# Stick-breaking attention in four steps, the tokens' memory attention beside the gate, and one more FFN part by block products

## The chip, the cores and the metric

One core of a Trainium2 chip runs the whole program. The metric is the device time of one execution in microseconds (us), and lower is better. TensorE (PE in the profile) does the matrix products and the transposes, VectorE (DVE) and ScalarE (ACT) the elementwise work, GpSimd (POOL) little; SyncE (SP) issues nearly all DMAs. Each engine runs its own instructions in a fixed order and waits at the first whose data or buffer is not ready.

## The reference

A decoder step of two layers with shared weights, for 1024 prompt tokens and 8 sample tokens, all in float32. Layer 0 mixes tokens with a gated linear recurrence (HGRN2), layer 1 with stick-breaking attention over keys and values that are projected after layer 0. Both have four heads of cross-attention to 256 memory tokens beside it, and a SwiGLU FFN of hidden width 2816.

```python
def swiglu(h, w_gu, w_down):
    gate, up = jnp.split(h @ w_gu, 2, axis=-1)
    return (jax.nn.silu(gate) * up) @ w_down

# stick-breaking, for a block of queries
z = einsum('bqhd,bkhd->bhqk', q, k) * scale + bias
log_keep = where(mask, log_sigmoid(-z), 0.0)
tail = cumsum(log_keep, axis=3, reverse=True) - log_keep
w = where(mask, exp(log_sigmoid(z) + tail), 0.0)
o = einsum('bhqk,bkhd->bqhd', w, v)

# memory attention
p = softmax(einsum('blhd,bmhd->bhlm', q, mk) * scale)
o = einsum('bhlm,bmhd->blhd', p, mv)

# each sub-layer: h = h + rmsnorm(sublayer(rmsnorm(h, g)), g')
```

The outputs are the tokens of both kinds after the two layers, the recurrent states, and the keys and values.

## The kernel before

Tokens lie along the free dimension. The prompt is done in two groups of 512; the second group takes the 8 sample tokens along, so that its tiles are 520 wide (as halves of 256 and 260 columns in the FFN). A float32 product is made of three: operand and weight are each split into a high and a low half (ACT casts, line L217 or L612; DVE subtracts, L218 or L614), and high x high, high x low and low x high are summed in PSUM. So each 512 columns of weights cost a DMA, a cast and a subtraction before PE can use them.

A scheduler sets the order of the instructions on each engine from the program's order and its buffers. The program's order is made by streams (generators) that `weave((stream, n), ...)` runs side by side, in proportion to the numbers n. `tc.issue_after` ties one instruction behind another.

The FFN's hidden width is done in five parts of 5, 5, 4, 4 and 4 slices of 128 columns (parts 0 to 4, so that the fourth part is part 3). A plain slice (`gate_up_q`, L545) takes 96 matmuls of half the group's width. In `ffn_w` a slice takes seven block products (`gate_up_w`, L619) in the way of Strassen, 84 matmuls, from sums of operand blocks (`sums_w`, done once for a group) and sums of weight blocks (made in DRAM by GpSimd's DMAs, `wsum`, or on the spot). The list `steps` given to `ffn_w` says how many slices stay plain, and how many steps of the operand sums go beside each of them. For the first group of layer 0 that list was (5, 6, 5): the first three slices of part 3 were plain, its last one and part 4 used block products.

Stick-breaking (`sb_prompt`) goes head by head over units of at most 512 scores by 128 queries, in steps: scores (L1594), softplus and reverse scan (L1580, L1581, L1614, L1616), the exponential of the weights (L1617), transposes of them (`turn`, L1623) and the values (L1634). One call of `step` begins a unit, turns the unit before it and takes the values of the one before that:

```python
old, turned = turned, asked and (*asked[0], *turn(*asked[1]))
asked = new
if old:
    values(*old)
```

Memory attention (`mem_attn`) has the same form with a softmax (L1051, L1019, L1032). The names in the profile: `ws` split weights, `w` and some `b` and `c` tiles raw weights, `x`, `a`, `y` split operands or their sums, `q` and `s` PSUM banks of FFN products and of small work (three banks), `m` the FFN's middle. Pool C holds four tiles of 2 x 512 columns, pool B seven of 512.

The stages that the change touches, with their times in the profile: samples' recurrence, gate and FFN part 1 of layer 0's first group (507 to 620 us); memory attention of the tokens and of the samples beside part 2 (to 700); parts 3 and 4 (to 865); layer 1 of the first group, stick-breaking and memory attention beside parts 0 and 1, some of them by block products (975 to 1195); layer 1 of the second group beside layer 0's FFN (1526 to 1840); and the end (from 2368).

## Time and profile before

| | us |
|---|---|
| median of 3 runs | 2404.62 (2404.50 to 2404.99) |
| the profiled execution, as the runs are timed | 2406.1 |
| its span, first to last instruction | 2404.4 |
| PE busy | 2377.7 (99%) |
| DVE busy | 1710.3 (71%) |
| ACT busy | 1322.5 (55%) |
| POOL busy | 113.7 (5%) |

The prediction quotes the page and its views word for word. In a row of groups stand line, engine, operation, the tile written <- the tiles read, the shape and a count; then the busy time and the mean duration of one in ns; then the idle time of the engine before them and what ended it. In a row of waits stand who waited for whom, the total in us, how often, and the longest. A timeline's row begins with start and duration in us.

### The profile page before, as it was taken

How to read it: one execution, taken by the hardware profiler on the slowest of the kernel's cores; microseconds unless marked ns; L12 is line 12 of the kernel's file. 1: busy time of each engine (PE TensorE's matmuls, PEld its weight loads, DVE VectorE, ACT ScalarE, POOL GpSimd, SP SyncE). 2: the span in 40 equal slices, each digit the busy share in tenths (PEclk: the TensorE clock that was granted, in tenths of full speed). 3: DMA queues.
4: the chain of work that ended last, by engine and by line, in shares of the span. 5: the costliest groups of instructions: out<-in, count | busy, mean ns of one | idle time of the engine just before them, and what ended most of it. 6: DMA issues, size and time to landing. Idle time of an engine off the chain costs nothing.

```text
span 2404.4 us, 42487 instructions
## 1 busy us (share of the span) xinstructions
PE 2377.7 (99%) x15962; PEld 2156.4 (90%) x15962; DVE 1710.3 (71%) x3195; ACT 1322.5 (55%) x2736; POOL 113.7 (5%) x187
## 2 busy tenths in 40 slices
PE   9999999999999999999999999999999999999998
PEld 7888989888889988999999989877778989999998
DVE  5867558766776676878556677777776679676866
ACT  5547544454664554667544554568457566554445
POOL 1001202100000000000001200111000000000000
PEclk9999999999999999999999999999999999999999
DMA  6454766677535447332659746545354354343342
GB/s 198 122 165 119 174 199 161 164 197 193 168 106 166 134 154 232 94 101 88 193 168 225 205 152 194 161 137 156 108 154 125 95 158 137 106 129 100 113 125 76
DMA packets 514641, 357.60 MB, mean 149 GB/s; under 512 B 20173, under 2 KB 463674, under 8 KB 514434
## 3 DMA queue, kind: packets, MB, share of 16 engines
q1 hardware_dynamic: 498562, 312.93, 43.8%
q0 software_dynamic: 15872, 41.95, 7.4%
q8 instruction: 126, 2.06, 0.4%
q14 instruction: 81, 0.66, 0.1%
HBM read 322.86 MB, written 65.49 MB: 162 GB/s over the span
## 4 chain that ended last, share of the span: by engine, by line
PE 85%; DVE 6%; ACT 4%; DMA 3%; issue 2%; SPq 0%; DVEq 0%; ACTq 0%
PE mm L231 37%; PE q L619 18%; PE q L791 11%; PE q L545 4%; PE mm L1235 2%; PE s L1414 1%; DMA b<-qd 1%; PE s L1051 1%; PE s L1032 1%; PE mm L968 1%; PE mm L995 1%; PE q L823 1%; DVE ws L218 1%; ACT c L1123 1%; DVE b L1614 1%
## 5 line engine op out<-in xcount | busy, mean ns | idle before, releaser
L231 PE MATMUL mm<-x,ws 128*128 128x512 f32 (+1 forms) x5016 | 924.4, 342 | 2.2 <-ACT a L1470 1.1
L231 PEld LDWEIGHTS mm<-x,ws 128*128 128x128 f32 x5016 | 774.8, 188 | 111.4 <-ACT a L1470 1.3
L217 ACT CAST ws<-w 128x512 fp32r<-128x512 f32 x596 | 346.6, 584 | 396.1 <-PE mm L231 228.4
L218 DVE TENSOR_TENSOR ws<-w,ws 128x512 fp32r<-128x512 f32 x596 | 381.1, 646 | 238.5 <-ACT ws L217 230.5
L791 PE MATMUL q<-m,ws 128*128 128x260 f32 (+1 forms) x2496 | 303.9, 283 | 0.1
L791 PEld LDWEIGHTS q<-m,ws 128*128 128x128 f32 x2496 | 299.9, 188 | 1.0 <-ACT m L238 0.3
L619 PE MATMUL q<-y,ws 128*128 128x260 f32 (+1 forms) x1920 | 249.3, 284 | 1.9 <-DVE t L654 1.7
L619 PEld LDWEIGHTS q<-y,ws 128*128 128x128 f32 x1920 | 237.6, 188 | 3.2 <-DVE t L654 1.9
L619 PE MATMUL q<-x,ws 128*128 128x260 f32 (+1 forms) x1668 | 219.7, 283 | 1.3 <-DVE ws L614 0.7
L619 PEld LDWEIGHTS q<-x,ws 128*128 128x128 f32 x1668 | 207.7, 188 | 2.2 <-DVE ws L614 1.1
L231 PE MATMUL mm<-m,ws 128*128 128x512 f32 x768 | 186.1, 396 | 0.0
L612 ACT CAST ws<-w 128x512 fp32r<-128x512 f32 x206 | 125.0, 619 | 96.8 <-PE q L791 30.8
L231 PEld LDWEIGHTS mm<-m,ws 128*128 128x128 f32 x768 | 142.9, 188 | 32.0
L614 DVE TENSOR_TENSOR ws<-w,ws 128x512 fp32r<-128x512 f32 x206 | 139.4, 688 | 44.9 <-ACT ws L612 41.6
L800 DVE TENSOR_TENSOR r<-r,q 128x260 f32<-128x260 f32 (+1 forms) x160 | 60.6, 420 | 46.8 <-PE q L791 46.5
L545 PE MATMUL q<-x,ws 128*128 128x260 f32 (+1 forms) x720 | 87.0, 282 | 0.0
L545 PEld LDWEIGHTS q<-x,ws 128*128 128x128 f32 x720 | 86.3, 188 | 0.2
L238 ACT CAST m<-t 128x512 fp32r<-128x512 f32 (+1 forms) x88 | 54.7, 622 | 37.5 <-DVE t L860 19.8
L612 ACT CAST ws<-b 128x512 fp32r<-128x512 f32 x82 | 50.6, 620 | 42.5 <-PE q L791 13.4
L614 DVE TENSOR_TENSOR ws<-b,ws 128x512 fp32r<-128x512 f32 x82 | 56.5, 689 | 20.6 <-ACT ws L612 19.9
L239 DVE TENSOR_TENSOR m<-t,m 128x512 fp32r<-128x512 f32 (+1 forms) x88 | 60.9, 691 | 13.5 <-ACT m L238 12.5
L290 DVE TENSOR_TENSOR st<-st,n 128x512 f32<-128x512 f32 (+1 forms) x91 | 62.3, 692 | 3.7 <-ACT n L289 2.2
(422 smaller groups left out, 3117.0 us busy)
## 6 DMA issues: line engine op xcount, KB each, us to landing
w<-in_w_gu SPq DMA_DIRECT2D x275, 256.0 KB
w<-in_w_down SPq DMA_DIRECT2D x160, 256.0 KB
wsum<-in_w_gu POOLq DMA_DIRECT2D x48, 512.0 KB, 6.1
w<-in_w_in_a SPq DMA_DIRECT2D x80, 256.0 KB
w<-in_w_o SPq DMA_DIRECT2D x64, 256.0 KB
w<-wsum SPq DMA_DIRECT2D x61, 256.0 KB
b<-in_w_gu SPq DMA_DIRECT2D x39, 256.0 KB
b<-wsum SPq DMA_DIRECT2D x39, 256.0 KB
```

What stands on the lines that cost most here:

```text
L217: nc.scalar.copy(ws[:, 0, :n, :], raw[:, :n, :])
L218: split[0] = nc.vector.tensor_sub(ws[:, 1, :n, :], raw[:, :n, :], ws[:, 0, :n, :].bitcast(F32))
L231: nc.tensor.matmul(ps[:, a, : PW[g]], wt, xt[k][:, xi, o : o + PW[g]], start=(k == 0 and wi == 0), stop=(k == nk - 1 and wi == 2),)
L238: nc.scalar.copy(dst[0], src)
L239: nc.vector.tensor_sub(dst[1], src, dst[0].bitcast(F32))
L290: nc.vector.tensor_add(acc[:, :n], acc[:, :n], t[:, :n])
L545: ins = nc.tensor.matmul(pp[a][:, :h], wt, xt[k][:, xi, a * h : (a + 1) * h], start=(k == 0 and wi == 0), stop=(k == ND - 1 and wi == 2),)
L612: nc.scalar.copy(w[:, 0, :], src)
L614: split[0] = nc.vector.tensor_sub(w[:, 1, :], src, w[:, 0, :].bitcast(F32))
L619: nc.tensor.matmul(ps[:, :h], w[:, wj, k * P : (k + 1) * P], x[:, xi, :], start=(first and k == 0 and wi == 0), stop=(k == 3 and wi == 2), ...
L791: nc.tensor.matmul(pp[a][:, :h], wt, mids[k][:, xi, a * h : (a + 1) * h], start=(k == 0 and wi == 0), stop=(k == nf - 1 and wi == 2),)
L800: nc.vector.tensor_add(d, d, pp[a][:, :h])
```

## The change

Six things:

- **Block products.** `ffn_w` of layer 0's first group gets the empty list: all four slices of part 3 now use block products. The operand sums stand beside part 2, where the memory attention was.
- **Memory attention of the tokens** in layer 0's second group goes one stage earlier, beside the samples' recurrence, the gate and part 1. Since the tiles for its result do not exist yet, it is parked in the key tiles (`parked`) and moved later (`unpark`). The samples' memory attention is woven 8 steps beside part 2 and 24 beside parts 3 and 4.
- **Stick-breaking** turns a unit one step later, and its e tile is half a C tile (`spare`) instead of a B tile.
- **The samples' recurrence** goes by four samples in one C tile, not by eight in two.
- **The end**: the first half of the output rows is turned after product 5 and not 7, the last product is scaled by DVE into a tile of its own, and the rows are stored in halves of 256 KB.
- **Loads and pacing**: two of the residual's tiles are fetched first and the others as they are needed, and the splits in `mixer_b.load` are tied behind the last weight split.

```diff
-        po, asked, turned = [None, None], None, None
+        po, asked, scored, turned, spare = [None, None], None, None, None, []
         def step(new=None):
-            nonlocal asked, turned
+            nonlocal asked, scored, turned
             old, turned = turned, asked and (*asked[0], *turn(*asked[1]))
-            asked = new
+            asked, scored = scored, new
...
-            e = B()
+            if not spare:
+                c = C()
+                spare.extend((c[:, 0], c[:, 1]))
+            e = spare.pop(0)
...
-        for h in range(H):
+        for h, a in ((h, a) for h in range(H) for a in range(2)):
...
-            for a in range(2):
-                qs = B(F32R), B(F32R)
-                split_to(qs, vb[:, a, :])
-                late.extend((h, a, i, p) for i, p in enumerate(qs))
+            qs = B(F32R), B(F32R)
+            split_to(qs, vb)
+            late.extend((h, a, i, p) for i, p in enumerate(qs))
...
+        def mem_parked(self):
+            yield from mem_attn(self.g, 0, self.Qm, lambda h, po: nc.scalar.copy(self.parked(h), po))
+
+        def unpark(self):
+            for h in range(H):
+                put(self.xo, H + h, slice(0, G), self.parked(h))
+                yield
...
-                    nc.scalar.activation(R, R, AF.Copy, scale=gcol(l, 3, m))
-                    if m == 7:
-                        list(rows.turn(0))
+                    if m < ND - 1:
+                        nc.scalar.activation(R, R, AF.Copy, scale=gcol(l, 3, m))
+                    else:
+                        rows.last = T()[:, :h]
+                        nc.vector.tensor_scalar(rows.last, R, gcol(l, 3, m), None, op0=ALU.mult)
+                    if m == 5:
+                        rows.first()
...
+                    if c < CH:
+                        t0 = G + c * P
+                        nc.sync.dma_start(y_prompt[0, t0 : t0 + P, s], yt[:, s])
...
+    weave((a1.sample(), 16), (a1.gate(), 4), (a1.mem_parked(), 11), (f0.part(1), 14), (w0, 9))
     a1.open()
-    weave((a1.sample(), 16), (a1.gate(), 4), (f0.part(1), 14), (w0, 9))
-
-    def rest():
-        yield from f0.part(2)
-        set_banks(True)
-        fw = ffn_w(0, 0, o0.x, (5, 6, 5), 3, False, f0.R)
-        yield from fw.part(3)
-        yield from fw.part(4)
-        f0.acc = fw.acc
-
-    weave((chain(a1.merge(), a1.mem()), 36), (ms, 74), (rest(), 33))
+
+    fw = ffn_w(0, 0, o0.x, (), 3, False, f0.R)
+    weave((chain(a1.merge(), a1.unpark(), fw.sums), 25), (islice(ms, 8), 8), (f0.part(2), 15))
+    set_banks(True)
+    weave((ms, 24), (chain(fw.part(3), fw.part(4)), 20))
+    f0.acc = fw.acc
...
-    weave((chain(b0.sb(), b0.mem()), 25), (chain(fw.part(0), fw.part(1)), 28))
+    weave((chain(b0.sb(), b0.mem()), 26), (chain(fw.part(0), fw.part(1)), 28))
...
-        (chain(b1.sb(), b1.mem()), 40), (chain(b1.sb_sample(), b1.mem_sample()), 76),
+        (chain(b1.sb(), b1.mem()), 41), (chain(b1.sb_sample(), b1.mem_sample()), 76),
```

How the order moves is shown at two places. The first is PE in layer 1 of the second group (from some 1540 us), where the stick-breaking's scores (`s<-a,a`) and transposes (`s<-ident,b`) stand among the products of layer 0's FFN (`mm<-x,ws`). Before:

```order
L1594 MATMUL s_17240<-a_17122,a_16525 128x512
L1623 MATMUL s_17250<-ident,b_17129 128x128 x4
L231 MATMUL mm_17274<-x_16902,ws_17266 128x512 x3
L231 MATMUL mm_17274<-x_16906,ws_17266 128x512 x3
L231 MATMUL mm_17274<-x_16970,ws_17266 128x512 x3
L231 MATMUL mm_17274<-x_16974,ws_17266 128x512 x3
```

And now, from the second unit's scores on:

```order
L1621 MATMUL s_17296<-a_17178,a_16581 128x512
L231 MATMUL mm_17322<-x_16958,ws_17314 128x512 x3
L231 MATMUL mm_17322<-x_16962,ws_17314 128x512 x3
L231 MATMUL mm_17322<-x_17026,ws_17314 128x512 x3
L231 MATMUL mm_17322<-x_17030,ws_17314 128x512 x3
L231 MATMUL mm_17322<-x_17095,ws_17319 128x512 x3
L231 MATMUL mm_17322<-x_17099,ws_17319 128x512 x3
L231 MATMUL mm_17322<-x_17163,ws_17319 128x512 x3
L231 MATMUL mm_17322<-x_17167,ws_17319 128x512 x3
L1621 MATMUL s_17354<-a_17178,a_16581 128x512
L1653 MATMUL s_17364<-ident,b_17185 128x128 x4
```

The transposes of a unit stood right behind the next unit's scores; now 24 products and another unit's scores lie between.

The second place is layer 1 of the first group, at its first slice by block products (about 1010 us). SP's queue there, before (`ksc` and `vsc` are a head's keys and values in DRAM, `c` the raw weights of that slice, which had been loaded by four DMAs some 25 rows ahead; the `c` rows here are for the slices behind it):

```order
L1654 DMA a_1766_10852<-ksc1_151 128x512
L212 DMA w_1737_10641<-in_w_gu 128x4x128
L1655 DMA a_1767_10853<-vsc1_155 128x512
L212 DMA w_1739_10646<-in_w_gu 128x4x128
L212 DMA w_1745_10715<-in_w_gu 128x4x128
L212 DMA w_1747_10720<-in_w_gu 128x4x128
L579 DMA w_1758_10813<-in_w_gu 128x4x128
```

And now, where the first loads of `c` stand behind the keys of head 2:

```order
L585 DMA w_1808_11028<-in_w_gu 128x4x128
L1684 DMA a_1830_11187<-ksc2_152 128x512
L585 DMA c_1711_10358<-in_w_gu 128x4x128
L585 DMA c_1712_10359<-in_w_gu 128x4x128 x2
L585 DMA c_1711_10358<-in_w_gu 128x4x128
```

The load of the keys `ksc2` goes into the tile that held head 0's keys, so it waits for the last scores of that head. The loads of the weights stood ahead of all keys and now stand behind that wait.

ACT at the same place, before (`ws_1763` is the slice's first weight):

```order
L530 ACTIVATE t_1713_10468<-t_1713_10468 128x520
L217 CAST ws_1748_10722<-w_1747_10720 128x512
L612 CAST ws_1763_10819<-c_1687_10296 128x512
L238 CAST m_1730_10619<-t_1713_10468 128x520
L1580 ACTIVATE b_1733_10627<-b_1732_10624 128x256
L1625 COPY b_1735_10638<-s_1734_10633 128x512
L1581 ACTIVATE b_1733_10627<-b_1733_10627 128x256
```

And now (`ws_1783` is that weight):

```order
L238 CAST m_1772_10840<-t_1757_10694 128x520
L1655 COPY b_1777_10859<-s_1776_10854 128x512
L1655 COPY b_1791_10923<-s_1790_10920 128x256
L1607 ACTIVATE c_1775_10848<-b_1774_10845 128x512
L1608 ACTIVATE c_1775_10848<-c_1775_10848 128x512
L1607 ACTIVATE c_1775_10848<-b_1789_10910 128x512
L1608 ACTIVATE c_1775_10848<-c_1775_10848 128x512
L618 CAST ws_1783_10870<-c_1711_10358 128x512
```

The cast of the first weight stood ahead of one unit's softplus; now it stands behind the copies of two transposed units and the softplus of two others.

More of the change, by code (lines that the diff above doesn't have):

```diff
@@ L422, in residual, with fetch @@
         ht = [xpool.tile([P, 2, w], F32, tag=f"x{g}", name=nm("ht")) for _ in range(ND // 2)]
-        for j in range(ND // 2):
+        def fetch(j):
             if first:
@@ L428, in residual @@
                 nc.sync.dma_start(ht[j], hs[g][:, 2 * j : 2 * j + 2, :n])
+        for j in range(ND // 2 if first else 2):
+            fetch(j)
         for k in range(ND):
+            if not first and k % 2 == 0 and k < 4:
+                fetch(k // 2 + 2)
             if first:
@@ L891, in __init__, with first @@
             self.yt = {}
-        def turn(self, i):
+        def first(self):
             for c, n in self.rows:
@@ L1005, in mem_values, with mem_attn @@
         yield
-    def mem_attn(g, l, qm, xo):
+    def mem_attn(g, l, qm, out):
         mkt, mv = C(), C()
@@ L1036, in values @@
             if pr:
-                put(xo, H + h, slice(0, G), po)
+                out(h, po)
         def step(new=None):
@@ L1519, in mem, with parked @@
         def mem(self):
-            yield from mem_attn(self.g, 0, self.Qm, self.xo)
+            yield from mem_attn(self.g, 0, self.Qm, lambda h, po: put(self.xo, H + h, slice(0, G), po))
+        def parked(self, h):
+            return self.K[h // 2][:, h % 2, :G]
+        def mem_parked(self):
[4 more added lines that the diff above has]
+                yield
         def mem_sample(self):
@@ L1659, in sb_prompt @@
                 yield
-        for _ in range(2):
+        for _ in range(3):
             step()
@@ L1702, in load @@
                 x = X(self.g)
-                split_to((x[:, 0, :n], x[:, 1, :n]), t)
+                with tc.issue_after(split[0].ins):
+                    split_to((x[:, 0, :n], x[:, 1, :n]), t)
                 self.xo.append(x)
@@ L1710, in mem @@
         def mem(self):
-            yield from mem_attn(self.g, 1, self.Qm, self.xo)
+            yield from mem_attn(self.g, 1, self.Qm, lambda h, po: put(self.xo, H + h, slice(0, G), po))
         def sb_sample(self):
```

71 lines of the change are left out of this document (37 added, 34 removed).

## The prediction

> **What bounds the kernel now.** The first page gives the engines.
>
> ```profile
> span 2404.4 us, 42487 instructions
> PE 2377.7 (99%) x15962; PEld 2156.4 (90%) x15962; DVE 1710.3 (71%) x3195; ACT 1322.5 (55%) x2736; POOL 113.7 (5%) x187
> PEclk9999999999999999999999999999999999999999
> PE 85%; DVE 6%; ACT 4%; DMA 3%; issue 2%; SPq 0%; DVEq 0%; ACTq 0%
> ```
>
> TensorE (PE) is busy in 99% of the span at full granted clock, and the chain that ended last is 85% PE. So there are two ways to a shorter time: fewer matmuls, and less of the 27 us (2404.4 - 2377.7) in which PE is not busy. The waits of PE, costliest first, say what those are:
>
> ```profile
> PE s L1623 <- ACT b L1617: 6.8, 8, 1.7
> PE s L157 <- DMA prow<-in_g_norm: 3.2, 1, 3.2
> PE q L619 <- DVE t L654: 1.7, 1, 1.7
> ...
> PE s L1019 <- DVE b L1068: 0.5, 1, 0.5
> ```
>
> The largest is the stick-breaking: eight times its transposes (L1623) wait for the exponential of the weights (L1617). The same view of windows 1526 to 1840 (second group) and 1005 to 1060 (first group) divides it:
>
> ```profile
> PE s L1623 <- ACT b L1617: 5.9, 6, 1.7
> ```
> ```profile
> PE s L1623 <- ACT b L1617: 0.9, 2, 0.5
> PE q L619 <- DVE ws L614: 0.2, 1, 0.2
> ```
>
> The timeline of one of these waits shows its chain:
>
> ```profile
> 1661.71 1.02 PE L1594 MATMUL s<-a,a 128*128 128x512 f32 x2
> 1661.74 1.27 DVE L1614 TENSOR_TENSOR_SCAN b<-b 128x128 f32<-128x128 f32 x2 [0.23 <-ACT b L1581]
> 1663.05 0.69 DVE L1616 TENSOR_TENSOR b<-b,b 128x512 f32<-128x512 f32 x1
> 1663.78 0.63 ACT L1617 ACTIVATE b<-b 128x512 f32<-128x512 f32 x1 [1.27 <-DVE b L1616]
> 1664.46 0.66 PE L1623 MATMUL s<-ident,b 128*128 128x128 f32 x4 [1.73 <-ACT b L1617]
> ```
>
> PE issues a unit's scores and then the transposes of the unit before, whose scan has only just been done. Last, the stages that the change rearranges (columns: the stretch, its length, busy time of PE, PEld, DVE, ACT, POOL):
>
> ```profile
> 621.00:700.00 79.00, 78.50 (x362) 63.11 (x361) 60.53 (x115) 59.43 (x158) 0.00 (x0) 1.00 0.43 130
> 700.00:865.00 165.00, 165.00 (x1375) 163.80 (x1375) 114.45 (x224) 84.27 (x164) 0.00 (x0) 1.00 0.48 144
> 1526.00:1840.00 314.00, 308.12 (x1473) 245.29 (x1472) 233.51 (x363) 191.95 (x424) 26.72 (x24) 1.00 0.46 139
> 2003.00:2078.00 75.00, 74.41 (x622) 74.00 (x621) 70.91 (x149) 41.13 (x80) 0.00 (x0) 1.00 0.36 109
> ```
>
> VectorE (DVE) and ScalarE (ACT) have room in all but the last, where DVE is busy 70.91 of 75.00 us and PE still loses only 0.6 us: a measure for a nearly full DVE.
>
> **The change part by part.** *Three slices by block products.* Three plain slices of 96 matmuls become slices of 7 x 12 = 84: 36 fewer.
>
> ```profile
> L619 PE MATMUL q<-a,ws 128*128 128x256 f32 x324 | 41.8, 282 | 0.4 <-DVE ws L614 0.3 <-ACT ws L612 0.2
> L545 PE MATMUL q<-x,ws 128*128 128x256 f32 x240 | 29.0, 282 | 0.0
> ```
>
> A plain one occupies PE for 29.0 / 240 = 0.121 us, so 36 x 0.121 = 4.3 us go. If each block-product matmul cost 41.8 / 324 = 0.129 us, three slices would gain 3 x (96 x 0.121 - 84 x 0.129) = 2.3 us only; but that group holds the waits named in its row, and from 700 to 865, where five such slices run, PE loses nothing. I take -4.3, bounds -4.3 and -2.3. Each new slice takes three more casts and subtractions and three more loads than a plain one; they are counted under the stage below.
>
> *Transposes one step later in the second group.* The transposes of a unit now come two scores after its own, with 24 more matmuls of 512 columns between (at twice 0.121 some 5.8 us, far over 1.7). All six waits should go: -5.9; bounds -5.9 and 0. What is late next there is nothing the view of that window shows. The e tiles now take halves of the four C tiles that the sample loaders also use: 0, bounds 0 and +2.
>
> *The first group of the second layer.* The same step takes away 0.9 + 0.2. But here the order changes for the worse. The loads of the first block-product slice's weights (c, line L585) now stand in SP's queue behind a load of keys that waits for PE's last scores of head 0; before, they were issued well ahead. In front of this slice PE now does four score groups in close order, and on ACT four softplus activations of two units stand before the first weight cast, on DVE their scans before its subtraction. Durations from before, by window 1005 to 1060:
>
> ```profile
> L1614 DVE TENSOR_TENSOR_SCAN b<-b 128x512 f32<-128x512 f32 x3 | 3.7, 1223 | 2.4 <-ACT b L1581 2.4
> L1616 DVE TENSOR_TENSOR b<-b,b 128x512 f32<-128x512 f32 x5 | 3.4, 687 | 0.1
> L1581 ACT ACTIVATE b<-b 128x512 f32<-128x512 f32 x5 | 3.2, 632 | 0.0
> L1607 DVE SCALAR_TENSOR_TENSOR b<-s,biasp,cap 128x128 f32<-128x128 f32 x9 | 3.1, 345 | 0.0
> L612 ACT CAST ws<-c 128x512 fp32r<-128x512 f32 x4 | 2.5, 616 | 4.2 <-PE q L545 4.2
> L1625 ACT COPY b<-s 128x512 f32<-128x512 f32 x4 | 2.3, 568 | 0.0
> L1605 DVE TENSOR_SCALAR b<-s,biasp 128x384 f32<-128x384 f32 x3 | 1.8, 614 | 1.0 <-PE s L1594 1.0
> ```
>
> Followed by hand from the last plain matmul (0 us), with a next instruction starting some 0.09 before the one ahead ends: two score groups and one group of transposes end at 1.3. The next transposes need ACT's copy (0.57), which stands behind the cast of the plain slice's result: 2.05, so 0.75 idle. The values need DVE's third scoring operation (0.61, 0.69, 0.35 in a row): 0.3 idle. PE has done its attention work at 3.45. The two units' scores are in SBUF at 2.5 and 3.45; ACT's four activations (0.63 each) end at 5.0 and the cast (0.62) at 5.5: 2.1 idle. The third matmul needs the low half; ahead of that on DVE are a scan (1.22), a product (0.69), two short operations, and the subtraction (0.69) ends at 6.95: 1.2 idle. The second weights come by the same queues at 9.07 and 10.3 (0.45 and 0.55), the third at 12.5 and 13.2 (0.3 and 0.4). Sum 6.05. So this place gives +6.0 - 1.1 = +4.9; bounds +1 (the queues run ahead of my walk) and +8.
>
> *Memory attention one stage earlier.* Beside gate and samples its waits (0.5) should go: that stage has PE work enough between its steps. -0.5, bounds -0.5 and +2, since the parked results add ACT copies and the sample sums hold one of three small banks.
>
> *Operand sums beside the third part.* The stretch has some 58 DVE operations of 512 columns (0.69), 48 of 256 (0.42) and 8 of 1024 (1.22): 70 us of durations, about 60 after overlaps of 0.09, beside 276 matmuls of 512 columns, 67 us. That is 90 to 92%, below the 94.5% (70.91 of 75.00) at which 0.6 us was lost. +0.6, bounds 0 and +5.
>
> *Entry to the fourth part, and the sample values beside it.* The softmax of the sample scores (a short chain DVE, ACT, DVE, PE, DVE) now stands in DVE's queue ahead of the third weights' subtraction; from the last wide matmul on, the reduction, the exponential and two short operations end at 2.4 us, the copy of their transposes at 3.75 and the subtraction (0.69) at 4.45, where PE arrives at 3.75: 0.7. Then the four slices hold 40 scalings of 128 columns, 26 weight casts, 8 casts of results and 20 activations on ACT: 40 x 0.30 + 34 x 0.53 + 20 x 0.30 = 36 us by the starts (durations less the overlap) in 4 x 84 x 0.121 = 41 us of PE. ACT's scalings (0.394) wait for DMA, as before:
>
> ```profile
> L1123 ACT ACTIVATE c<-c,ss x128: 385/394/429, 646.7 to 1858.9; 128x128 f32<-128x128 f32 x128
> ...
>   DMA c<-in_cache_mem_v: 11.1, 7
> ```
>
> The weight tiles let ACT fall several products (1.4 us each) behind before PE sees it. I take +1 for this besides the 0.7; bounds 0 and +10.
>
> *The end.* Timeline of the last work, and the stores:
>
> ```profile
> 2394.92 1.04 PE L897 MATMUL s<-ident,r 128*128 128x128 f32 x8
> 2395.12 0.42 DVE L828 TENSOR_TENSOR r<-r,q 128x256 f32<-128x256 f32 x1
> 2395.55 0.58 ACT L902 COPY yT<-s 128x512 f32<-128x512 f32 x1 [0.46 <-PE s L897]
> 2397.81 0.75 DVE L926 SCALAR_TENSOR_TENSOR yT<-yT,rr,hT 128x512 f32<-128x512 f32 x1 [2.27 <-ACT rr L921]
> 2399.25 1.65 SPq L934 DMA_DIRECT2D out_y_prompt<-yT  x2
> 2399.80 0.74 DVE L929 SCALAR_TENSOR_TENSOR yT<-s,rr,hT 128x512 f32<-128x512 f32 x1
> GB/s 0 0 0 0 0 0 0 0 0 0 0 70 421 421 374 445 398 398 398 328 421 374 421 374 398 421 328 0 0 0 0 0 0 0 0 0 0 0 0 0
> ```
>
> Eight transposes move ahead of the last two products (+0.9 on PE, by the eight in 1.04), and the two copies that held up ACT after the last product (0.58 each) are gone: about -0.8 on the chain from 2395.12 to 2397.81. The last store carries 256 KB instead of 512: at 400 GB/s, 0.65 less. Together -0.6, bounds -1.2 and +0.6. The Trainium skill (DMA: Bandwidth & Descriptors, Bandwidth) speaks against this part: it says to batch transfers to 1 MiB and lists 0.95 us for 64 KB and 6.15 for 1 MB. Estimated on that line, two halves cost 4.0 us instead of 3.4, and the last store alone 2.0; if the stores queue the sum is 0.6 worse, if not 0.8 better. The trace does not show so large a price for size: two stores of 512 KB keep about 400 GB/s.
>
> **Sum.** -4.3 - 5.9 + 4.9 - 0.5 + 0.6 + 0.7 + 1.0 - 0.6 = -4.1 us. The profiled execution took 2406.1 us by the clock that times runs, 1.7 over its span, and 1.5 over the median of 2404.62; the durations belong to the span, and I set the difference against the median: 2400.5 us.
>
> **The rivals.** *No stall at the first block-product slice* (25%). For it: before, the same engines did the same work with 1.1 us lost, the walk is a sum of short overlaps, and DVE may reach that place early. Against: the loads stand behind a wait for PE whatever DVE does. Then -4.1 - 4.9 = -9.0: 2395.6 us.
>
> *ScalarE bound in the fourth part* (17%), the one that ends slower. Each block of sample values needs a 512 KB load, whose wait on ACT was 11.1 / 7 = 1.6 us; those scalings now stand ahead of weight casts that PE waits for, and the loads share C tiles with these weights, so a late cast makes the next load late. Eight such blocks at 1.6 us are 12.7 instead of 1.0: -4.1 + 11.7 = +7.6, 2412.2 us. It decides (over +4.8) from 8.9 + 1.0 = 9.9 us, 1.24 us for each block. For it: ACT at 36 of 41 us has no example above (59.43 of 79.00 is the fullest). Against: before, the weights' buffers hid such waits.
>
> *The waits in the second group stay* (10%), because ACT's queue and not the step is what is late: in the timeline ACT idled 1.27 us before the exponential, which speaks against it. -4.1 + 5.9 = +1.8: 2406.4 us.
>
> **Numbers.** The forecast's own sum has 40%, the other 8% are mixtures. A measurement of this kernel tells about 0.2%, 4.8 us, from no change: 2399.8 is the limit of faster, 2409.4 of slower. The forecast lies just inside no change; with terms that are uncertain by 3 us, 18 of its 40% fall on the faster side. With 24 of the first rival that is 42% faster. Slower: 15 of the second rival, 3 of the third, 3 of the rest: 21%. That leaves 37%. The range from 2392.5 to 2410.5 takes in the first rival with 3 us below it and most of the way to the second; 2 in 10 are left out, most of it above.
>
> **What would show it.** In the profile after: PE waits on the exponential of the weights gone from the second group's stick-breaking (under 0.5 us of 5.9); a cluster of PE waits of 4 to 8 us on casts and subtractions (L618, L620) at the first block-product slice near 1010 us; PE at 99% or more from 700 to 740; under 2 us waiting there for sample values. The prediction is wrong if the cluster near 1010 is missing, if the fourth part of the first layer takes 5 us more than its matmuls, or if the six waits are still there.

## The result and the profile after

| | before | after |
|---|---|---|
| median, same chip (6 runs each) | 2406.59 us | 2417.99 us |
| ratio, with its 95% interval | | 1.0046 [1.0035, 1.0056] |
| span of the profiled execution | 2404.4 us | 2416.8 us |

The change makes the kernel slower, by 11 to 12 us; the forecast was 4.1 us less. From the page of the changed kernel, and from its view of PE's waits:

```profile
span 2416.8 us, 42448 instructions
PE 2381.6 (99%) x15926; PEld 2158.4 (89%) x15926; DVE 1718.9 (71%) x3228; ACT 1330.8 (55%) x2756; POOL 113.7 (5%) x187
```
```profile
PE q L625 <- ACT ws L618: 5.2, 6, 1.7
PE s L1034 <- ACT b L1077: 3.8, 1, 3.8
PE q L625 <- DVE ws L620: 3.3, 7, 1.1
...
PE mm L231 <- ACT b L1647: 2.1, 1, 2.1
```

The 36 matmuls are gone (15962 to 15926), and so are the waits for the exponential of the weights (6.8 us before). In their place PE waits for block products' weights (L618, L620), 8.5 us, and once 3.8 us in the tokens' memory attention (L1034).

To see all of PE's loss and not only its longer waits, one more number is worked out from the trace: for every matmul the time from its start to the next one's start, less the median of that time for its line and shape; only the matmuls that took longer than that are counted. The sum over a stretch is called the *excess* below. It holds waits, slow clock and changes of shape.

| stretch (us) | what is in it | before | after | difference |
|---|---|---|---|---|
| 500 to 620 | recurrence, gate; now also the tokens' memory attention | 0.4 | 9.2 | +8.8 |
| 620 to 690 | part 2 | 1.4 | 2.1 | +0.7 |
| 690 to 880 | parts 3 and 4 | 2.3 | 8.8 | +6.5 |
| 1000 to 1080 | first group of layer 1, entry to block products | 3.1 | 6.8 | +3.7 |
| 1520 to 1860 | second group of layer 1 | 11.3 | 9.2 | -2.1 |
| 2060 to end | | 3.3 | 3.2 | -0.1 |
| all others | | 37.2 | 36.6 | -0.6 |
| sum | | 59.0 | 75.9 | +16.9 |

With 4.3 us of matmuls less, +16.9 makes +12.6; the spans differ by 12.4. So the table holds the whole loss, and three places carry it. (The stretches are the same in both columns. The changed kernel runs up to 15 us behind, and what is named lies inside its stretch in both.)

**500 to 620 us.** Four rows of the timeline of after:

```profile
560.92 0.37 SPq L1325 DMA_DIRECT2D c<-in_state_hgrn  x1
...
567.43 0.69 DVE L1350 TENSOR_TENSOR c<-c,a 128x512 f32<-128x512 f32 x1 [4.78 <-DMA c<-in_state_hgrn]
...
569.25 0.68 DVE L1071 TENSOR_REDUCE nmx<-s 128x2 f32<-128x512 f32 x1
...
571.68 1.12 PE L1034 MATMUL s<-ident,b 128*128 128x128 f32 x4 [3.77 <-ACT b L1077]
```

The load of the samples' recurrent states is issued at 560.92 and DVE has it at 567.43, 6.5 us later. DVE stands at its product for 4.78 us. Behind that product stands the maximum of the memory attention's softmax (L1071), and PE waits for what follows. The kernel before has no such wait of DVE in this stage: its last state was loaded 23 us ahead of its product, as its timeline shows:

```profile
536.45 0.37 SPq L1308 DMA_DIRECT2D c<-in_state_hgrn  x1
...
559.44 1.22 DVE L1332 TENSOR_TENSOR c<-c,a 128x1024 f32<-128x1024 f32 x1
```

So the change shortened the lead of this load: SyncE stood 3.0 us at it for a tile that was not yet free, and pool C has four tiles, of which the memory attention now holds two here. The stretches of after (columns as in the prediction; the last three are granted clock, DMA share, GB/s):

```profile
562.00:568.00 6.00, 5.91 (x33) 4.82 (x31) 1.22 (x2) 0.62 (x1) 0.00 (x0) 1.00 0.92 291
...
570.60:577.40 6.80, 5.72 (x27) 5.72 (x28) 3.83 (x8) 3.22 (x9) 0.00 (x0) 0.50 0.38 109
```

Two things are to be seen: the DMA engines are 92% busy while the state is under way, and PE's granted clock falls to 0.50 for 6.8 us after the wait. Of the kernel before, the rows for the same place:

```profile
550.00:556.00 6.00, 6.00 (x31) 4.63 (x30) 4.31 (x7) 2.73 (x6) 1.17 (x2) 1.00 1.08 321
556.00:562.00 6.00, 6.00 (x48) 5.79 (x48) 4.43 (x7) 2.92 (x6) 0.00 (x0) 1.00 0.93 299
```

There the engines were as full, but DVE waited for no state. The 9.2 us are 3.9 of wait, 2.7 in the slow matmuls right behind it, and 2.6 in pieces of 0.1 to 0.2 us, whose cause was not followed.

**690 to 880 us.** The same stretch before and after; then the waits of PE and of ACT in after, 690 to 800 and 700 to 800:

```profile
690.00:880.00 190.00, 189.50 (x1517) 184.59 (x1516) 135.15 (x261) 102.13 (x202) 0.00 (x0) 1.00 0.45 135
```
```profile
690.00:880.00 190.00, 184.31 (x1439) 176.48 (x1438) 135.98 (x253) 115.44 (x257) 0.00 (x0) 1.00 0.58 171
```
```profile
PE q L625 <- ACT ws L618: 3.6, 3, 1.7
PE q L625 <- DVE ws L620: 0.9, 3, 0.5
```
```profile
...
ACT ws L618 <- DMA b<-in_w_gu: 4.1, 3, 2.1
...
ACT ws L618 <- DMA b<-wsum: 3.7, 6, 1.1
...
ACT c L1138 <- DMA c<-in_cache_mem_v: 2.3, 1, 2.3
```

PE was idle for 0.5 us of 190 and now is for 5.7. It waits for casts of weights, and ACT waits for the loads of those weights (7.8 us) more than for the sample values (2.3).

**1000 to 1080 us.** The first slice by block products, in the timeline of after:

```profile
1029.88 0.63 ACT L1608 ACTIVATE c<-c 128x512 f32<-128x512 f32 x1
1030.41 0.60 ACT L618 CAST ws<-c 128x512 fp32r<-128x512 f32 x1
...
1031.07 0.51 PE L625 MATMUL q<-x,ws 128*128 128x260 f32 x2 [1.28 <-ACT ws L618]
...
1032.68 1.47 PE L625 MATMUL q<-x,ws 128*128 128x260 f32 x10 [1.10 <-DVE ws L620]
```

This is the walk of the prediction: the last of four softplus activations ends just ahead of the first cast, and PE stands there twice.

**1520 to 1860 us.** The waits of PE in the second group, the rows around the longer one, and the stretch behind it:

```profile
PE mm L231 <- ACT b L1647: 2.1, 1, 2.1
PE mm L231 <- DVE r L461: 0.9, 1, 0.9
```
```profile
1756.00 1.23 DVE L1113 TENSOR_TENSOR c<-c,b 128x1024 f32<-128x1024 f32 x1 [0.75 <-DMA b<-qd]
...
1758.57 3.81 PE L231 MATMUL mm<-x,ws 128*128 128x512 f32 x9 [2.10 <-ACT b L1647]
```
```profile
1758.40:1761.80 3.40, 3.23 (x8) 2.58 (x9) 3.40 (x6) 1.12 (x3) 0.00 (x0) 0.50 0.30 80
```

All six old waits are gone. One new wait of 2.1 us stands beside the samples' memory scores (L1113), which wait for DMA, and the clock falls to 0.50 for 3.4 us after it.

### The profile page after: what moved, and what is told of

The parts are those of the page before. It is cut to its first block, busy times and chain, and to the rows that moved or that the text cites. A ratio compares the mean times of both kernels' runs of the same rounds, so it can differ in the third digit from the quotient of the medians.

```text
span 2416.8 us, 42448 instructions
## 1 busy us (share of the span) xinstructions
PE 2381.6 (99%) x15926; PEld 2158.4 (89%) x15926; DVE 1718.9 (71%) x3228; ACT 1330.8 (55%) x2756; POOL 113.7 (5%) x187
## 4 chain that ended last, share of the span: by engine, by line
PE 90%; DVE 3%; DMA 3%; ACT 2%; issue 1%; SPq 0%; DVEq 0%; ACTq 0%
PE mm L231 40%; PE q L625 18%; PE q L797 12%; PE q L551 2%; PE mm L1250 2%; PE s L1430 1%; PE s L1664 1%; PE s L1621 1%; PE s L1047 1%; PE s L1066 1%; PE mm L983 1%; PE mm L1010 1%; PE q L829 1%; PE s L1034 1%; DMA b<-qd 1%
## 5 line engine op out<-in xcount | busy, mean ns | idle before, releaser
L625 PE MATMUL q<-x,ws 128*128 128x260 f32 (+1 forms) x1776 | 234.5, 283 | 6.2 <-ACT ws L618 2.9
L625 PEld LDWEIGHTS q<-x,ws 128*128 128x128 f32 x1776 | 221.4, 188 | 8.0 <-ACT ws L618 3.2
L618 ACT CAST ws<-w 128x512 fp32r<-128x512 f32 x217 | 131.6, 619 | 93.8 <-PE q L797 28.0
L620 DVE TENSOR_TENSOR ws<-w,ws 128x512 fp32r<-128x512 f32 x217 | 146.8, 688 | 40.2 <-ACT ws L618 38.0
L620 DVE TENSOR_TENSOR ws<-b,ws 128x512 fp32r<-128x512 f32 x92 | 63.3, 688 | 21.7 <-ACT ws L618 20.9
L618 ACT CAST ws<-b 128x512 fp32r<-128x512 f32 x92 | 56.7, 620 | 37.8 <-PE q L625 9.0
L625 PE MATMUL q<-a,ws 128*128 128x256 f32 x468 | 62.0, 283 | 3.8 <-ACT ws L618 2.1
L625 PEld LDWEIGHTS q<-a,ws 128*128 128x128 f32 x468 | 57.7, 188 | 6.7 <-ACT ws L618 3.5
```

The costliest lines, as they stand in the source:

```text
L618: nc.scalar.copy(w[:, 0, :], src)
L620: split[0] = nc.vector.tensor_sub(w[:, 1, :], src, w[:, 0, :].bitcast(F32))
L625: nc.tensor.matmul(ps[:, :h], w[:, wj, k * P : (k + 1) * P], x[:, xi, :], start=(first and k == 0 and wi == 0), stop=(k == 3 and wi == 2), ...
```

## The experiments

Seventeen kernels. A kernel's ratio is against the kernel before, run on the same chip; for the changed kernel it is 1.0046. The excess is that of the stretch named, from one profiled execution: where kernels do not differ in a stretch, it still differs by some 2 us (8.4 to 10.8 us from 690 to 880 in the five kernels with the changed kernel's parts 3 and 4).

### The wait at 571 us

*Sums later*: the last nine steps of the weight sums (GpSimd's DMAs) no longer beside the recurrence, but beside the projections of layer 1.

```diff
-    weave((a1.sample(), 16), (a1.gate(), 4), (a1.mem_parked(), 11), (f0.part(1), 14), (w0, 9))
+    weave((a1.sample(), 16), (a1.gate(), 4), (a1.mem_parked(), 11), (f0.part(1), 14))
...
-    weave((b0.heads(), 8), (o1.finish(), 17))
+    weave((b0.heads(), 8), (o1.finish(), 17), (w0, 9))
```

> The changed kernel with the last nine steps of GpSimd's weight sums moved from the stage of samples and gate (507 to 620 us) to the stage before layer 1's first stick-breaking. In the changed kernel a state load there took from 560.9 to 567.4 us, DVE waited 4.8 us for it, PE 3.8 us for the exponential behind it, and the granted clock fell to 0.71 for some 10 us. Theory (transfers): the load is slow because the sums and the weights fill the DMA engines; without the sums it lands in under 4 us, PE's wait falls under 1 us, the clock stays at 1.00 and the kernel gains 5 to 7 us. Rival (tiles): the load is issued late, since the parked memory attention's keys and values leave two of the four C tiles to the states; then it still comes late, PE's wait stays over 2 us, and at most 3 us are gained.

Ratio 1.0021 [1.0011, 1.0031]; excess from 500 to 620 3.5 us instead of 9.2. From its waits and its stretches:

```profile
PE s L1034 <- ACT b L1077: 0.4, 1, 0.4
```
```profile
568.00:574.00 6.00, 5.59 (x46) 5.37 (x46) 3.97 (x10) 3.37 (x10) 0.00 (x0) 1.00 0.36 98
```

Wait and slow clock are gone with the transfers. The state is issued as late as in the changed kernel (561.82), but its product starts at 564.96, after 3.1 us instead of 6.5, and DVE waits 1.4 us for it. The fifteen kernels with the new recurrence agree: the six that have the sums elsewhere show 3.0 to 3.1 us from issue to product and a wait of PE of 0.3 to 0.4 us, the nine with the sums here 4.9 to 6.5 and 2.2 to 3.8. So it is the state's load beside the sums' transfers, not DVE's work, that made the wait. The late issue is the other half of it, and what made that, the memory attention's two C tiles or the recurrence's smaller steps, no run tells apart.

### Parts 3 and 4

Seven runs ask what costs 6.5 us here. *Plain slices* (`fw = ffn_w(0, 0, o0.x, (0, 0, 0), 3, False, f0.R)`, three slices of part 3 plain, nothing else moved) and *split weights not in C tiles* (part 3 left out of the rule that puts three of eight split weights into C tiles):

> The changed kernel with the first three slices of layer 0's part 3 in the first group plain again (36 matmuls more), the operand sums and all else where the change put them. Theory (block products beside sample values): the 6 us of PE waits on weight casts between 707 and 742 us go, 4.3 us of matmuls come back, and the kernel gains 1 to 3 us. Rival (the sample values alone, or the sums beside part 2, are the cause): the waits stay at 4 us or more, and the kernel loses 3 to 5 us.

> The changed kernel with none of part 3's split weights in pool C, so that the loads of the samples' values find all four of its tiles, while the split weights have five tiles instead of up to eight. Theory (tiles): ACT's waits for these loads (2.3 us at 726 us) and PE's 4.3 us on casts from 725 to 742 us fall under 1.5 us, and the kernel gains 2 to 4 us. Rival (ScalarE's and the weights' own load): with less room for split weights the waits stay or grow, and the kernel is the same or loses up to 4 us.

Plain: 1.0038 [1.0023, 1.0052], excess 7.7; the waits went from part 3, which has no wait left, to the entry of part 4, where block products begin (two of 1.2 and 0.9 us, and the clock at 0.50 for 6.8 us behind the second). C tiles: 1.0035 [1.0022, 1.0047], excess 10.3; no help. So the three slices are not the cause by themselves, and neither are the C tiles.

*Samples beside part 2*: all 32 steps of the samples' memory attention beside part 2, parts 3 and 4 alone.

```diff
-    weave((chain(a1.merge(), a1.unpark(), fw.sums), 25), (islice(ms, 8), 8), (f0.part(2), 15))
+    weave((chain(a1.merge(), a1.unpark(), fw.sums), 25), (ms, 32), (f0.part(2), 15))
...
-    weave((ms, 24), (chain(fw.part(3), fw.part(4)), 20))
+    drain(fw.part(3), fw.part(4))
```

> The changed kernel with all of the samples' values beside part 2 and the operand sums, and none beside parts 3 and 4. Theory (the values' scalings and loads beside block products make the waits there): of the 8.8 us that PE loses between 690 and 880 us 6 go, part 2 loses at most 2 with DVE full, and 3 to 6 us are gained. Rival (DVE): sums, values and weight splits together are more than PE's time in part 2, the loss moves there, and the time is the same or longer.

Ratio 1.0062 [1.0045, 1.0079]. Part 2 with sums, merge and samples overfills DVE (13.00 busy of 13.00 us from 655 to 668), and one wait there is the longest:

```profile
PE mm L231 <- DVE ws L218: 3.9, 1, 3.9
```

The excess from 690 to 880 is 10.0 us and not the 3 that were expected, but 8.6 of it lie ahead of 726 us, where the last samples are. From there on the block products of parts 3 and 4 wait 0.2 us in all up to 800. They can run nearly without loss; it is what stands beside them.

*One load* (the first layer's sample values loaded once for eight blocks), *no scaling* (ACT's scalings left out) and *no values* (both):

```diff
+            if once and kept:
+                return kept[0]
             t = C()
...
-            for k in range(2):
+            for k in range(2 if scaled else 0):
```

> The changed kernel, with the sample values of the first layer loaded once and used for all eight blocks (seven of eight loads are left out, so seven blocks use the wrong values). It asks what costs the 6.5 us in parts 3 and 4 (690 to 880 us: 8.8 us beyond the matmuls, 2.3 before). Theory A, the loads: they share C tiles and DMA queues with the weights, so without them the waits for DMA on ScalarE (4.1 + 3.7 + 2.3 us from 700 to 800) mostly go and the stretch falls from 8.8 to 4 us or less. Theory B, ScalarE's own work: 40 scalings stand ahead of weight casts whatever the loads do, and the stretch stays at 7.5 to 9.

> The changed kernel without the scalings of the sample values in the first layer (ScalarE's activations by the sample's softmax sum are left out there, the loads stay, so that the products take unscaled values). Theory B (ScalarE's own work): with some 40 x 0.30 = 12 us less on ScalarE beside 41 us of PE, the stretch from 690 to 880 falls from 8.8 to 4 us or less. Theory A (the loads): it stays above 7, with ScalarE still waiting for weights' loads.

> The changed kernel with both left out in the first layer: seven of eight loads of the sample values and all their scalings (so the sample's attention there is not computed). One alone left the stretch from 690 to 880 at 9.5 and 8.3 us (8.8 in the changed kernel). Theory A+B, two causes side by side, each enough to make the weights late: without both the waits between 720 and 745 (3.3 us of the excess) go, under 1 us, and the stretch falls to about 5; what stays is the softmax's 1.4 us near 707 and the 1.8 at the last step near 794. Rival: the seven weights for each slice come late by SyncE's queue whatever stands beside them: 3 us stay.

Excess 9.5, 8.3 and 10.3 us, about what this stretch has without these edits: none of the three helps, and theories A, B and A+B fall. (Ratios 1.0041 [1.0025, 1.0057], 1.0052 [1.0031, 1.0072], 1.0031 [1.0020, 1.0041]; no values gains at other stretches.) The rival of the last one held. From 700 to 760 us of *no values* ACT still waits for the weights, and SyncE's queue suggests why (the first view is ACT's waits, the second SyncE's, the third its timeline):

```profile
ACT ws L618 <- DMA b<-wsum: 5.3, 3, 3.1
ACT ws L618 <- DMA b<-in_w_gu: 5.1, 2, 3.6
```
```profile
SPq L585 <- DVE t L660: 6.9, 1, 6.9
```
```profile
719.90 0.50 SPq L585 DMA_DIRECT2D b<-wsum  x1
727.01 0.36 SPq L585 DMA_DIRECT2D w<-wsum  x1
727.41 1.06 SPq L585 DMA_DIRECT2D b<-wsum  x2
```

For 7 us SyncE stands at one load into a `w` tile that DVE has not given free, and the loads into `b` tiles stand behind it. They are issued in a bunch when they are already wanted; that sets DVE back, and the next `w` tile comes free late again. This is read from the trace and not shown by a run: none alters the queue here, and in the kernel before SyncE stands up to 5.9 us at a load in the same stretch and PE waits for nothing. What of the values' remaining steps (adds, casts, `b` tiles, products) holds the queue was not told apart.

*Values beside the down products*: the sample values not beside gate and up slices, but beside the down products of parts 3 and 4. It is built on *two undone*, which has sums later and the e tile in a B tile again.

```diff
-    weave((ms, 24), (chain(fw.part(3), fw.part(4)), 20))
+    p3, p4 = fw.part(3), fw.part(4)
+    weave((islice(p3, 9), 9))
+    weave((islice(ms, 14), 14), (p3, 4))
+    weave((islice(p4, 9), 9))
+    weave((ms, 10), (p4, 4))
```

> The changed kernel with two places undone: e tiles in B tiles again, and the last nine steps of the weight sums moved from the recurrence's stage to the projections of layer 1. Singly they gave 1.0031 and 1.0021 where the changed kernel has 1.0046. If the places add up, the stretches lose 5.7 + 3.8 us: excess about 66, ratio 1.000 to 1.002. If the moved sums make a wait of their own between 880 and 1000, as one run with three edits had it (8.8 us there), the ratio is 1.003 or more.

> As two_undone, and the sample values beside the down products of parts 3 and 4 instead of the gate and up slices by block products. Theory: a slice by block products needs seven loads, casts and subtractions for 84 matmuls, and has no room beside it for the sample values; a down product has. Then the stretch from 690 to 880 falls from 8.8 to about 4 us and the ratio to 0.998 to 1.000. Rival: the last step's casts and the softmax hold the weights up wherever they stand, and the scalings do the same beside the down products: 7 us or more, ratio no better than two_undone.

Two undone: 1.0032 [1.0021, 1.0044], excess 9.7 from 690 to 880. Values down: 1.0011 [1.0002, 1.0021], excess 5.5. PE's waits from 700 to 745 of the one and of the other:

```profile
PE q L625 <- ACT ws L618: 2.0, 2, 1.0
PE q L625 <- ACT q L637: 1.3, 2, 1.0
PE q L625 <- DVE ws L620: 0.9, 3, 0.5
PE q L625 <- DVE r L461: 0.7, 1, 0.7
```
```profile
PE q L625 <- DVE r L461: 0.9, 1, 0.9
```

So the values' steps cost some 4 us more beside block-product slices than beside the down products. The ratio of 0.998 to 1.000 that was expected of *values down* was missed by a wait at another place, which *two undone* has too, from 880 to 1000 us (excess 8.1 instead of 2.7):

```profile
PE ns L279 <- ACT n L238: 3.8, 1, 3.8
```

The moved sums do not make it alone: *sums later*, with the sums at the same place, has no wait there and an excess of 2.8, and *e in B* (below) has 2.6. It stands in the three kernels that have both.

### Entry to block products in layer 1

*e in B*: the e tile is a B tile again, with the four steps kept. *Keys by GpSimd*: the first group's keys and values loaded from GpSimd's queue. *Before with four steps*, with the e tile in B and in C: the kernel before with the new step alone.

```diff
-            if not spare:
-                c = C()
-                spare.extend((c[:, 0], c[:, 1]))
-            e = spare.pop(0)
+            e = B()
```
```diff
-            nc.sync.dma_start(kh[:, : g + 1, :G], ksc[h][:, : g + 1, :])
-            nc.sync.dma_start(vh[:, : g + 1, :G], vsc[h][:, : g + 1, :])
+            q = nc.sync if g else nc.gpsimd
+            q.dma_start(kh[:, : g + 1, :G], ksc[h][:, : g + 1, :])
+            q.dma_start(vh[:, : g + 1, :G], vsc[h][:, : g + 1, :])
```

> The changed kernel with the stick-breaking's e tile in pool B again, the extra step kept. In the order the first block-product slice's weight loads of layer 1's first group then stand ahead of all keys again. Theory (tiles in C): the waits at that slice (6.5 us more than the matmuls from 1025 to 1065 us, 3.0 in before's) fall to 3 us or less, and in the second group the waits of 1748 to 1761 us (5 us with the low clock) go, since the samples' loads have all of pool C; 7 to 9 us gained. Rival (the extra step itself, or pool B's seven tiles, makes the waits): they stay or others of that size take their place, under 3 us gained.

> The changed kernel, with the keys and values of the first group's stick-breaking loaded from GpSimd's queue and not SyncE's, so that the weights' loads are no longer behind a load that waits for PE. ScalarE's and VectorE's orders stay. The prediction's walk puts the stall at the first block-product slice (1000 to 1080: 6.8 us against 3.1) on ScalarE's and VectorE's order: it stays at 6 to 7 us. The rival, the wait in SyncE's queue: it falls to 3 to 4 us, as before.

> The kernel before with one part of the change alone: the stick-breaking's transposes one step later, the e tile left in pool B. Theory: the 6.8 us of waits for the exponential of the weights go and nothing takes their place, so 5 to 7 us are gained. Rival (the waits move): DVE and ACT finish a unit no sooner, and waits elsewhere in these two stages take back all but 1 to 3 us.

> As the run with the later transposes alone, but with the e tile in halves of C tiles, as the change has it. Theory (tiles in C): the first block-product slice of layer 1's first group waits 3 to 4 us longer, since its weights' loads fall behind the keys, and in the second group the samples' loads come late for 3 to 5 us; the kernel is within 2 us of before. Rival (C tiles are not the cause): as the run with e in pool B, to within 2 us.

Keys by GpSimd: 1.0051 [1.0031, 1.0071], excess from 1000 to 1080 6.8 us, as in the changed kernel. SyncE's timeline and PE's waits of that run:

```profile
1009.43 2.47 SPq L585 DMA_DIRECT2D c<-in_w_gu  x4
```
```profile
PE q L625 <- DVE ws L620: 1.5, 2, 1.1
PE q L625 <- ACT ws L618: 1.5, 2, 1.3
```

The weights are loaded 14 us earlier than in the changed kernel (1026.60 there; this run has come 3 us earlier to the place), and the waits are the same to 0.1 us. So SyncE's queue is not what holds them; the orders on ACT and DVE are. With the e tile in B the excess is 3.6 (ratio 1.0031 [1.0019, 1.0044]), and ACT has the first casts from 1013 us on, ahead of the softplus. In the kernel before with the new step, the excess is 10.7 with the e tile in C and 3.0 with it in B; PE's waits of the C version:

```profile
PE q L791 <- ACT m L238: 1.9, 1, 1.9
PE q L619 <- ACT ws L612: 1.3, 1, 1.3
PE q L619 <- DVE ws L614: 1.1, 1, 1.1
```

It is the choice of tile that moves the casts, not the new step. All other kernels with the new step agree: an excess of 6.6 us or more here with e in C, 3.0 to 3.6 with it in B. The same choice made the new wait of the second group near 1757 us: the ten kernels with e in C have one of 1.5 to 2.6 us there, and the eight with it in B have none over 0.4.

The new step alone is worth its price: *before with four steps* has a ratio of 0.9984 [0.9974, 0.9994], 2402.56 us beside 2406.13, the lowest ratio here (e in C: 0.9991 [0.9981, 1.0001]). Its excess from 1520 to 1860 is 7.7 us, 3.6 less than before; with the e tile in B the changed kernel too has 8.1 there and no wait over 1.4.

### Do the places add up?

A first run with e in B, sums later and samples beside part 2 only joined the last one's new wait to that of the sums:

> The changed kernel with three parts altered together: GpSimd's last weight sums later, the e tile in pool B, the samples' values beside part 2. If the three causes are separate, the gains add: 6 + 3.6 + 3 to 6, so 13 to 16 us less than the changed kernel and 2 to 5 less than before. If one wait hides behind another, less than 10 us are gained and it stays slower than before.

Ratio 1.0052 [1.0035, 1.0068], excess 10.6 from 620 to 690 and 8.8 from 880 to 1000. Then *values down* with the sums moved to part 2 or to the gate and up slices of part 4 (`weave((islice(p4, 9), 9), (w0, 9))`):

> As values_down, with the last nine steps of the weight sums beside part 2 (620 to 700 us, DMA share 0.48) instead of the projections of layer 1. values_down loses 8.2 us from 880 to 1000, most of it one wait of 3.6 on ScalarE's cast there and what follows it. If that wait comes from the moved sums' transfers, it goes: 880 to 1000 at 2.5 to 3 us, ratio 0.998 to 1.000, which with 36 matmuls fewer is at or below the kernel before. If not: the ratio stays at 1.001 and the wait is there.

> As sums_part2, but with those nine steps beside the gate and up slices of part 4 (770 to 810 us, DMA share 0.79). Same theory for 880 to 1000: 2.5 to 3 us. For 690 to 880 it tells whether block-product slices bear more DMA beside them: over 7 us (5.5 in values_down) if their weights are at the edge, and no change if the queue of loads and not the DMA engines is what makes them late.

Ratios 1.0003 [0.9994, 1.0012] and 1.0001 [0.9992, 1.0010], excess from 880 to 1000 2.9 and 2.6: the wait of 3.6 us is gone in both. From 690 to 880 they have 4.9 and 6.3 us, with 5.5 in *values down*: below the 7 us that were set as the mark, and too close to tell what transfers beside the block products cost. The page of the second:

```profile
span 2404.0 us, 42478 instructions
PE 2377.1 (99%) x15926; PEld 2154.0 (90%) x15926; DVE 1717.9 (71%) x3228; ACT 1333.6 (55%) x2758; POOL 115.3 (5%) x187
```

Its excess is 63.1 us, 12.8 below the changed kernel's, and its span is 12.8 shorter. Three edits of place, with all the work kept, give back the loss. Against the kernel before the span is 0.4 us less, where the forecast had 4.1; what is missing lies in 500 to 620 (3.3, before 0.4) and 690 to 880 (6.3, before 2.3), less some gains elsewhere.

Last, *before with four steps* and one more slice by block products, `ffn_w(0, 0, o0.x, (8, 8), ...)`:

> The kernel before with the four-step stick-breaking alone (e in a B tile, as in the run before_four: 0.9984) and the list (8, 8) in place of (5, 6, 5): one more slice of the first layer's first group by block products, 12 matmuls fewer, and no other part of the change. If block products pay as long as their sums and samples leave ScalarE and VectorE room: 12 x 0.121 = 1.5 us less than before_four, ratio about 0.998, the stretch from 690 to 880 at 2 to 2.5 us. If operand sums at eight steps a slice already hold PE up: 690 to 880 at 4 us or more and no gain over before_four.

Ratio 0.9992 [0.9982, 1.0001], excess from 690 to 880 2.7. The 12 matmuls (1.5 us) cannot be seen in the time, and the interval overlaps that of four steps alone: not decided.

## Why the prediction was wrong

It failed in three terms, whose misses make 17.9 us; the other terms and stretches come to 1.2 us less than forecast.

- **Block products, -4.3**: right, 36 matmuls at the same pace.
- **Transposes one step later, -5.9**: the mechanism was right (no such wait is left, and in the kernel before it alone took 3.6 us off the stretch). "What is late next there is nothing the view of that window shows" holds for the step alone and not for the change: the wait of 2.1 us and the slow clock behind it come with the e tile in C tiles, whose term was "0, bounds 0 and +2". With the tile in B the stretch has 1.1 us less, which is within what one stretch varies by. Measured -2.1, inside the bounds of the first term. Why the step alone gave 3.6 and not 5.9 stays open.
- **First group of the second layer, +4.9**: right in mechanism and place; measured +3.7. Of the walk's waits at that slice the first came out at 1.28 beside 2.1 and the second at 1.10 beside 1.2; the later ones, 1.7 together, hardly came (0.6). That the sum of waits is lower and the term so near is in part luck. The first cause it named, the loads behind a wait in SyncE's queue, was no cause (keys by GpSimd); the second, the order on ACT and DVE, was. The prediction puts that order down to the new step; it comes with the e tile in C tiles (3.2 us less at this place with it in B).
- **Memory attention one stage earlier, -0.5, bounds -0.5 and +2**: the step that failed most, by 9.3 us. "that stage has PE work enough between its steps" looked at PE and not at what shares DVE's queue there: the recurrence's products, which need loads, at a place where the DMA engines were 92 to 108% busy. And the sum has no term at all for the recurrence's new form and for the two C tiles that the memory attention takes from it: the state that had been issued 23 us ahead was now issued 6.5 us ahead. So a load wait that was not there before stood ahead of a softmax that PE waits for. The DMA share of 1.08 and 0.93 from 550 to 562 us stood in the trace of the kernel before.
- **Operand sums, +0.6**: right (+0.7).
- **Entry and sample values, +0.7 and +1.0**: +6.5, 4.8 more than the sum and inside the bounds of 0 to +10. "The weight tiles let ACT fall several products (1.4 us each) behind before PE sees it" failed: PE saw it, with 5.7 us of idling. That the place of the values' steps, beside block-product slices, makes some 4 us of the stretch's loss is shown; that they do so by tiles given back late and loads issued late is what one trace suggests. The rival *ScalarE bound in the fourth part* had the place and the sign right, but neither of its two mechanisms: ACT's work and the value loads can both be left out, and the loss stays.
- **The end, -0.6**: 0. The chain from DVE's last FFN sum to the end of the span is 1.1 shorter (9.28 to 8.17 us, 0.7 of that behind DVE's last operation, where the stores are), but the eight transposes ahead of it put that sum off by 1.2 (27.5 to 28.7 us from the start of the last part's down products). The store's share was right (-0.65 forecast). By the Trainium skill (DMA: Bandwidth & Descriptors, Bandwidth) the prediction had an estimate of 0.6 us more if the stores queue; the trace does not bear that out, since what follows DVE's last operation went from 3.9 to 3.1 us. DVE's first and last step of that chain in after:

```profile
2408.63 0.42 DVE L834 TENSOR_TENSOR r<-r,q 128x256 f32<-128x256 f32 x1
...
2412.26 1.40 DVE L946 SCALAR_TENSOR_TENSOR yT<-s,rr,hT 128x512 f32<-128x512 f32 x2
```

As for what would show it: the six waits are gone, and the cluster near 1010 us is there (at 1030, with 3.0 us instead of 4 to 8). PE was busy for 36.15 of the 40 us from 700 to 740, 90% instead of 99%; parts 3 and 4 took some 5 us more than their matmuls, which for the fourth part had been named as what makes the prediction wrong. What no term held was the clock. The slow matmuls behind the waits of 3.8 and 2.1 us add 2.6 us to the first and 1.6 to the second.

## What to carry to other kernels

When a step is moved to where "PE has work enough", list what stands ahead of it in the queues of DVE, ACT and SyncE at the new place, and above all which of that needs a load and how far ahead the load is issued: a wait for it is charged to the newcomer's consumers. Count the tiles that the step takes with it, since a load that has to wait for one is issued late. Read the DMA share of the new place before moving anything that depends on a load, or a load itself. Which tile a new value lives in can matter more than the step that makes it, since it decides where the order lets later loads and casts go.

## What the runs showed of the hardware

- The granted clock fell to 0.50 after some short waits of PE, for 3.4 or 6.8 us: for 6.8 behind one of 3.8 us (at 571) and for 3.4 behind one of 2.1 (at 1758). In *sums later* it was 0.50 from 791.0 to 794.4 us behind a single wait of 1.6 us, in *plain slices* from 804.0 to 810.8 behind waits of 0.3 and 0.9 within two microseconds. In the kernel before, with waits of up to 1.7 us, every five microseconds between 20 and 2395 us show 1.00. So the length of one wait does not tell it alone. Of PE's wait of 3.1 us at the very start nothing can be said, since the traces of these two kernels hold no clock before 9.7 us. The Trainium skill (TensorE: Matmul & The Clock Gate, HAM oscillation — how this bites in real kernels) gives about 3.4 us of idling as the rule; here one wait of 1.6 was enough, and no run shows where the limit is.
- A load of 256 KB took 6.5 us from issue to use where DMA engines were 92% busy, and 3.1 us at the same place at 47% (*sums later*).
- Executions of the kernel before, over all comparisons, went from 2400.7 to 2409.9 us without any change in it, so 0.2% takes many runs to tell.
